# Attention scores on the two row halves of TensorE, a pair's probabilities side by side, and a reordered mixer

## The chip, the cores and the metric

The kernel runs on one core of a Trainium2 chip. The metric is the device time of one execution in microseconds, the median over several runs. One execution was also taken by the hardware profiler; its page, its timeline and its chain of waits are what the prediction reads.

## The reference

The kernel computes two layers of an encoder trunk on 256 tokens of width 1024, all in float32, and a final RMSNorm. Each layer is

```
x += 1/2 SwiGLU_a(RMSNorm(x))
u  = RMSNorm(x) @ W_in          -> q, k, v (512 each), hy (3 * 512)
y_A = neighbourhood attention(q, k, v)      8 heads x 64, bias and mask, softmax
y_B = x0 * long_conv(hv * x1)               512 channels, through a spectrum
x += [RMSNorm(y_A); RMSNorm(y_B)] * g_out @ W_out
x += 1/2 SwiGLU_b(RMSNorm(x))
x += sigmoid(RMSNorm(x) @ W_g) * (p[i] @ W_p)
```

The change lies in the third to fifth line, called the mixer below. For one head of 64 channels the attention computes scores q k^T (256 x 256) times 1/8, adds a bias that is -1e30 outside the neighbourhood, takes a softmax over the keys, and multiplies with v.

## The kernel before

**Products.** Every float32 operand is split into a high part and a rest (`split`, L207: ScalarE rounds, VectorE subtracts), and one product is three matmuls: high by high, high by rest, rest by high. `mm3` (L166 to L170) issues them into one PSUM bank; `Wide.mm` (L187) does the same in the feed-forward parts with one 512-column and one 256-column matmul. Weights stream from HBM: each half piece is loaded, rounded by ScalarE (L281) and its rest taken by VectorE (L283), some six half pieces ahead of their use. Activations lie transposed, channels on partitions and the 256 tokens along the free axis.

**Order of work.** TensorE and ScalarE run in the order in which the program issues instructions; the order on VectorE and GpSimd is a planner's. Side work (normalising, softmax, splitting) stands in generators called fibers. `paced` (L172) counts matmul triples in units of 256 columns; at each third unit `tick` (L150) steps every live fiber once, newest first. `yield` and `rest(n)` in a fiber let it sleep 1 or n ticks. `finish` (L134) ticks until a fiber is done, with no matmul issued in between. So the number of counted units decides between which matmuls a fiber's own TensorE and ScalarE instructions are placed.

**The mixer** (L669). First v for all heads (`vps`, two banks, tokens on partitions). Then the blocks of `ORDER` (L55) one after another. `g`, `q` and `x` are blocks of two products of eight triples each (`columns`, L673), 16 counted units: q and k of a pair of heads, or inputs of the convolution. The others are

- `s` scores of a pair: for each of its two heads two triples (L758). The contraction runs over all 128 partitions; the head's q is padded with zeros in the other head's 64 partitions (`QK`, L718: `qh`, `ql`, zeroed by GpSimd), so the other head's k drops out.
- `t` turn: eight 128 x 128 transposes of the probabilities (L787), one bank per head, then a split per head.
- `p` attend: per head and per half of the keys one triple of 256 columns (L821), four triples into one bank; v is padded with zeros in the other head's columns (`values`, L697).
- `u` turns the convolution's input, `f` is its forward transform with the product in the spectrum (`spectral`, L894), `i` the transform back.

At the end `project` multiplies with W_out in two halves m = 0, 1 of the output channels. A fiber of `Turned` (L952) forms `w` on VectorE (L964, two token halves) and then issues eight transposes on TensorE (L971) into banks, from which VectorE adds to x (L976); `prep` then scales and splits x into the next block's inputs `xg` (L363, L365). The next feed-forward begins at once with `Wide.mm` over its inputs c = 0 to 7, four 512-column matmuls (L188) for each c and, after every second c, eight 256-column ones (L197). c = 0 to 3 come from m = 0, c = 4 to 7 from m = 1; so the eight transposes of m = 1 fall among the first L188 matmuls of that feed-forward.

Of the kernel before, what the change touches and what calls it, by code (L numbers as in the profile page):

```python
# [54 lines left out]
ORDER = "g0 q0 g1 s0 q1 g2 t0 s1 g3 q2 t1 p0 u0 q3 f0 s2 f1 p1 s3 t2 x0 x1 t3 i0 p2 p3 i1 i2 i3"  # L55
MIXER = [(t[0], int(t[1])) for t in ORDER.split()]

# [20 lines left out]
def hybrid_trunk(ctx: ExitStack, tc: tile.TileContext, w, xT, pT, rpb, small, gfin, wf, zT, dft, idft, decay, out):  # L78
# [590 lines left out]
    def mixer(i):  # L669
# [24 lines left out]
        vh = [[t2(F32R, "vh") for _ in range(2)] for _ in range(2)]  # L694
        vl = [[t2(F32R, "vl") for _ in range(2)] for _ in range(2)]

        def values():  # L697
            for tt in range(2):
                for pp in range(2):
                    G.memset(f(vh[tt][pp]), 0.0)  # L700
                    G.memset(f(vl[tt][pp]), 0.0)
            yield from rs.wait()
            for tt in range(2):
                vf = t2()
                V.tensor_scalar(vf, vps[tt], rs.r[:, tt : tt + 1], None, op0=ALU.mult)
                yield
                for pp in range(2):
                    src = vf[:, pp * 256 : (pp + 1) * 256].rearrange("p (a b c) -> p a b c", a=2, b=2)
                    hv, lv = v2(vh[tt][pp]), v2(vl[tt][pp])
                    for par in range(2):  # L710
                        cs = slice(par * 192, par * 192 + 64)
                        S.copy(hv[:, :, cs], src[:, :, par])
                    yield
                    for par in range(2):
                        cs = slice(par * 192, par * 192 + 64)
                        V.tensor_sub(lv[:, :, cs], src[:, :, par], f(hv[:, :, cs]))

        class QK:  # L718


            def __init__(self, b):
                self.kh, self.kl = t1(F32R), t1(F32R)
                self.qh, self.ql = t2(F32R), t2(F32R)
                self.fb = spawn(self.go(b))

            def go(self, b):
                G.memset(f(self.qh), 0.0)
                G.memset(f(self.ql), 0.0)
# [5 lines left out]
                where = [  # L734
                    (slice(64 * par, 64 * par + 64), slice(T * par, T * par + T)) for par in range(2)
                ]
# [619 lines left out]
```

## Time and profile before

| | us |
|---|---|
| median of 3 runs | 1078.4 (1078.39 to 1078.43) |
| the profiled execution | 1078.43, span 1076.7 |
| TensorE (PE) busy | 1057.3 (98%), 6442 matmuls |
| VectorE busy | 876.0 (81%) |
| ScalarE busy | 659.0 (61%) |
| GpSimd busy | 131.1 (12%) |
| mean granted TensorE clock | 0.997 of full speed |

The span is the time between the first and the last instruction of the profile; the execution's own time is 1.7 us longer. The matmuls are pipelined: a row's duration is the time of one from start to end, several are under way at once, and what one costs in a row of them is the distance from one start to the next. The first mixer's blocks run from 211.55 to 297.7 us, the second's from 740.5 to 827.1 us.

### The profile page before, as it was taken

To read this page: it belongs to the slowest core of one execution; us is meant where nothing else is said; L and a number is where in the kernel's file an instruction comes from. 1 tells how busy PE (TensorE), PEld (TensorE's weight loads), DVE (VectorE), ACT (ScalarE), POOL (GpSimd) and SP (SyncE) were. 2 spreads that over 40 slices of the span, in tenths; PEclk is the share of its full clock that TensorE was granted. 3 is DMA by queue.
4 is the path that set the end of the run, shared out by engine and by line. 5 is a ranking of instruction groups with operands and counts; after the bars stand their busy time and mean duration, and the time that the engine had idled before them with its cause. 6 is when DMAs were issued, how large, how long until landed. Compare 5 with 4: busy or idle time off the path is not lost.

```text
span 1076.7 us, 17162 instructions
## 1 busy us (share of the span) xinstructions
PE 1057.3 (98%) x6442; PEld 947.9 (88%) x6442; DVE 876.0 (81%) x1562; ACT 659.0 (61%) x1198; POOL 131.1 (12%) x138
## 2 busy tenths in 40 slices
PE   7999999999999999999999999999999999999996
PEld 6888888899988888888988888889999788888885
DVE  5999878798988877676889888899989887776765
ACT  7566665476766656555667665655767665665553
POOL 3000111511212000010110001223131300000100
PEclk9999999999999999999999999999999999999998
DMA  8666545454345555545465654545523555555541
GB/s 325 212 232 235 197 157 195 176 198 156 118 166 170 187 191 195 196 162 197 152 217 187 234 196 162 191 156 185 198 89 111 177 190 197 182 180 186 173 160 40
DMA packets 33411, 194.54 MB, mean 181 GB/s; under 512 B 3632, under 2 KB 6832, under 8 KB 11312
## 3 DMA queue, kind: packets, MB, share of 16 engines
q1 hardware_dynamic: 33328, 193.44, 51.7%
q8 instruction: 51, 0.84, 0.3%
q14 instruction: 32, 0.26, 0.1%
HBM read 192.38 MB, written 1.05 MB: 180 GB/s over the span
## 4 chain that ended last, share of the span: by engine, by line
PE 94%; DVE 3%; ACT 2%; issue 1%; DMA 0%; SPq 0%; DVEq 0%; ACTq 0%
PE ps L188 44%; PE ps L197 23%; PE ps L167 8%; PE ps L169 8%; PE ps L168 8%; DVE wl L283 1%; DVE xg L365 1%; PE ps L787 1%; ACT wh L281 0%; PE ps L413 0%; DMA raw<-in_w 0%; ACT t L780 0%; DVE x L1076 0%; PE ps L971 0%; DVE s L1075 0%
## 5 line engine op out<-in xcount | busy, mean ns | idle before, releaser
L283 DVE TENSOR_TENSOR wl<-raw,wh 128x1024 fp32r<-128x1024 f32 (+1 forms) x350 | 430.6, 1253 | 105.0 <-PE ps L197 51.5
L281 ACT CAST wh<-raw 128x1024 fp32r<-128x1024 f32 (+1 forms) x350 | 363.4, 1042 | 184.5 <-PE ps L188 90.2
L188 PE MATMUL ps<-xg,wh 128*128 128x512 f32 x1408 | 344.6, 393 | 8.2 <-DVE xg L1195 6.5
L188 PEld LDWEIGHTS ps<-xg,wh 128*128 128x128 f32 x1408 | 258.5, 189 | 58.4 <-DVE xg L1195 6.8
L197 PEld LDWEIGHTS ps<-xg,wl 128*128 128x128 f32 x1408 | 182.4, 192 | 7.7
L197 PE MATMUL ps<-xg,wl 128*128 128x256 f32 x1408 | 184.6, 283 | 0.0
L188 PE MATMUL ps<-act,wh 128*128 128x512 f32 x704 | 173.0, 391 | 0.0
L188 PEld LDWEIGHTS ps<-act,wh 128*128 128x128 f32 x704 | 128.2, 189 | 23.9
L351 POOL TENSOR_TENSOR acc<-acc,q 128x256 f32<-128x256 f32 x56 | 55.9, 999 | 532.1 <-ACT q L348 395.7
L167 PE MATMUL ps<-xg,wh 128*128 128x256 f32 x384 | 109.0, 284 | 0.0
L169 PE MATMUL ps<-xg,wl 128*128 128x256 f32 x384 | 108.7, 283 | 0.0
L168 PE MATMUL ps<-xg,wh 128*128 128x256 f32 x384 | 108.7, 283 | 0.0
L197 PEld LDWEIGHTS ps<-act,wl 128*128 128x128 f32 x704 | 92.9, 191 | 5.1
L197 PE MATMUL ps<-act,wl 128*128 128x256 f32 x704 | 94.4, 282 | 0.0
L202 ACT COPY gu<-ps 128x256 f32<-128x256 f32 x176 | 56.4, 375 | 45.1 <-PE ps L197 45.0
L167 PEld LDWEIGHTS ps<-xg,wh 128*128 128x128 f32 x384 | 73.7, 192 | 0.1
L168 PEld LDWEIGHTS ps<-xg,wh 128*128 128x128 f32 x384 | 73.7, 192 | 0.1
L169 PEld LDWEIGHTS ps<-xg,wl 128*128 128x128 f32 x384 | 73.7, 192 | 0.0
L205 DVE TENSOR_TENSOR gu<-gu,ps 128x256 f32<-128x256 f32 x176 | 66.1, 414 | 0.0
L500 DVE TENSOR_TENSOR act<-s,act 128x256 fp32r<-128x256 f32 x88 | 36.6, 424 | 33.1 <-ACT act L498 32.5
L363 ACT ACTIVATE xg<-x,sm 128x256 fp32r<-128x256 f32 x56 | 27.0, 506 | 35.8 <-DVE x L529 24.3
L365 DVE SCALAR_TENSOR_TENSOR xg<-x,sm,xg 128x256 fp32r<-128x256 f32 x56 | 30.2, 558 | 12.6 <-ACT xg L363 12.4
(209 smaller groups left out, 1236.8 us busy)
## 6 DMA issues: line engine op xcount, KB each, us to landing
raw<-in_w SPq DMA_DIRECT2D x172, 1024.0 KB, 4.9
bias<-in_rpb SPq DMA_DIRECT2D x16, 256.0 KB, 2.7
raw<-in_w SPq DMA_DIRECT2D x4, 256.0 KB, 4.5
x<-in_xT SPq DMA_DIRECT2D x8, 128.0 KB, 4.7
raw<-in_w SPq DMA_DIRECT2D x2, 512.0 KB, 5.7
t<-in_wf SPq DMA_DIRECT2D x4, 256.0 KB, 5.5
dec<-in_decay SPq DMA_DIRECT2D x4, 256.0 KB, 5.5
out<-yo SPq DMA_DIRECT2D x3, 256.0 KB, 2.1
```

Of the source, the lines that this page charges most:

```text
L167: PE.matmul(o, lh, rh, start=start, stop=False)
L168: PE.matmul(o, lh, rl, start=False, stop=False)
L169: PE.matmul(o, ll, rh, start=False, stop=stop)
L188: PE.matmul(b, lh, r, start=start, stop=False)
L197: PE.matmul(o, ll, rh, start=False, stop=stop)
L202: S.copy(dst, b[:, T:])
L205: V.tensor_add(dst, dst, b[:, :T])
L281: S.copy(h[:, a : a + k], src)
L283: V.tensor_sub(l[:, a : a + k], src, f(h[:, a : a + k]))
L351: G.tensor_add(self.ac, self.ac, q)
L365: V.scalar_tensor_tensor(hl[:, T:], x[c], g, f(hl[:, :T]), op0=ALU.mult, op1=ALU.subtract)
L500: V.tensor_sub(hl[:, T:], s, f(hl[:, :T]))
```

## The change

- **Scores.** q and k are no longer padded. A pair's two heads stay in partitions 0 to 63 and 64 to 127, and each matmul contracts over 64 partitions: the two heads' matmuls alternate and write two banks. There are still 12 matmuls of 256 columns for a pair, and the block counts two units instead of four.
- **Turn and attend.** The transposes put the two heads' probabilities side by side, one bank per half of the keys. `attend` multiplies a pair's 128 columns of v with 512 columns of probabilities, six matmuls instead of twelve, and only the two diagonal blocks of the result (64 x 256 each) are copied out by ScalarE before `head_norm`.
- **Values and QK** split 512 columns at once; the zeroing on GpSimd and the small copies go.
- **Spectrum.** One yield less after each pair of multiplications and one less between the GpSimd combination and its split.
- **Order.** The blocks stand in another order, and s0 and s1 now run between the two products of q1 and q2. s2 stands right behind q3, and t2 behind x0.
- **The end.** `rest(1 + m)`: the transposes of m = 1 come one tick later.

```diff
-ORDER = "g0 q0 g1 s0 q1 g2 t0 s1 g3 q2 t1 p0 u0 q3 f0 s2 f1 p1 s3 t2 x0 x1 t3 i0 p2 p3 i1 i2 i3"
+ORDER = "g0 q0 g1 q1+s0 g2 g3 t0 q2+s1 p0 u0 q3 s2 t1 f0 f1 p1 s3 x0 t2 x1 t3 p2 i0 p3 i1 i2 i3"
...
+                S.activation(vh[tt], vps[tt], AF.Copy, scale=r)
+                yield
+                V.scalar_tensor_tensor(vl[tt], vps[tt], r, f(vh[tt]), op0=ALU.mult, op1=ALU.subtract)
...
-                S.copy(self.kh, q[:, T:])
-                for r, c in where:
-                    S.copy(self.qh[r, c], q[r, :T])
-                yield
-                V.tensor_sub(self.kl, q[:, T:], f(self.kh))
-                for r, c in where:
-                    V.tensor_sub(self.ql[r, c], q[r, :T], f(self.qh[r, c]))
+                S.copy(self.h, q)
+                yield
+                V.tensor_sub(self.l, q, f(self.h))
...
-                    mm3(b[:, tt * T : (tt + 1) * T], st.qh[:, qs], st.ql[:, qs], st.kh, st.kl, True, True)
+            banks = [bank(), bank()]
+            for tt in range(2):
+                qs = slice(tt * P, (tt + 1) * P)
+                for n, (a, b) in enumerate(((st.h, st.h), (st.h, st.l), (st.l, st.h))):
+                    for par, o in enumerate(banks):
+                        r = slice(64 * par, 64 * par + 64)
+                        PE.matmul(o[:, tt * T : (tt + 1) * T], a[r, qs], b[r, T:], start=n == 0, stop=n == 2)
+                paced()
...
+            for kt in range(2):
+                b = bank()
+                for h in hs:
+                    h.fb.finish()
+                    for tt in range(2):
+                        o = T * h.par + tt * P
+                        PE.transpose(b[:, o : o + P], h.e[:, tt * T + kt * P : tt * T + (kt + 1) * P], ident)
...
+            for kt, (h, l, fb) in enumerate(ps):
+                fb.finish()
+                vs = slice(128 * pair, 128 * pair + 128)
+                mm3(b, vh[kt][:, vs], vl[kt][:, vs], h, l, kt == 0, kt == 1)
...
+                for par in range(2):
+                    r = slice(64 * par, 64 * par + 64)
+                    S.copy(y[r], b[r, T * par : T * par + T])
...
                 p.append((m, p0, p1))
                 yield
-                yield
...
                 yield
                 yield
-                yield
                 S.copy(yf[m][0], p0)
...
-                yield
+                yield from rest(1 + m)
                 self.banks = [bank(), bank()]
```

## Rows read from the trace of the kernel before

**Rows 1.** The page's first part: engine, busy us, share of the span, instructions.
```profile
PE 1057.3 (98%) x6442; PEld 947.9 (88%) x6442; DVE 876.0 (81%) x1562; ACT 659.0 (61%) x1198; POOL 131.1 (12%) x138
```
**Rows 2.** The page's chain of work that ended last: share of the span by engine.
```profile
PE 94%; DVE 3%; ACT 2%; issue 1%; DMA 0%; SPq 0%; DVEq 0%; ACTq 0%
```
**Rows 3.** Who waited for whom, TensorE alone, the whole span: us in total, times, longest.
```profile
PE ps L188 <- DVE xg L365: 1.8, 2, 1.0
PE ps L971 <- DVE w L964: 1.5, 2, 1.0
```
**Rows 4.** Stretches of 15 us of the first mixer: length, then busy us (instructions) of PE, PEld, DVE, ACT, POOL, then the granted TensorE clock, the DMA share and GB/s.
```profile
220.00:235.00 15.00, 15.00 (x127) 15.00 (x127) 14.91 (x28) 10.67 (x21) 1.21 (x2) 1.00 0.59 216
...
265.00:280.00 15.00, 14.86 (x101) 13.35 (x100) 14.14 (x27) 9.72 (x28) 5.83 (x5) 1.00 0.42 141
```
**Rows 5.** Timeline of TensorE, the scores of the first pair: the first of its 12 matmuls, and the first matmul behind them. Columns: start us, us, engine, line, operation, out<-in, weights, moving operand, count.
```profile
229.06 0.28 PE L167 MATMUL ps<-s,t 128*128 128x256 f32 x1
...
230.50 0.28 PE L167 MATMUL ps<-xg,wh 128*128 128x256 f32 x1
```
**Rows 6.** Timeline of TensorE, the transposes of the first pair (eight, merged into a row) and the two matmuls behind them.
```profile
242.02 1.04 PE L787 MATMUL ps<-ident,t 128*128 128x128 f32 x8
242.81 0.36 PE L167 MATMUL ps<-s,t 128*128 128x256 f32 x1
243.02 0.28 PE L168 MATMUL ps<-s,t 128*128 128x256 f32 x1
```
**Rows 7.** Timeline of TensorE: two 512-column matmuls three apart, then the first of the second pair's 12 matmuls with v and the first matmul behind them.
```profile
266.24 0.39 PE L167 MATMUL ps<-t,dft_h 128*128 128x512 f32 x1
...
266.92 0.39 PE L167 MATMUL ps<-t,dft_h 128*128 128x512 f32 x1
...
271.78 0.28 PE L167 MATMUL ps<-t,vh 128*128 128x256 f32 x1
...
273.22 0.28 PE L167 MATMUL ps<-s,t 128*128 128x256 f32 x1
```
**Rows 8.** Timeline of TensorE around the transposes of the third pair, in the first and in the second layer.
```profile
274.67 1.74 PE L787 MATMUL ps<-ident,t 128*128 128x128 f32 x8
276.17 0.36 PE L167 MATMUL ps<-xg,wh 128*128 128x256 f32 x1
...
803.54 0.28 PE L169 MATMUL ps<-s,t 128*128 128x256 f32 x1
803.94 1.92 PE L787 MATMUL ps<-ident,t 128*128 128x128 f32 x8
805.61 0.36 PE L167 MATMUL ps<-xg,wh 128*128 128x256 f32 x1
```
**Rows 9.** Timeline of ScalarE just there, second layer: the four scalings of the third pair's probabilities.
```profile
803.38 1.87 ACT L780 ACTIVATE t<-t,ri 128x256 f32<-128x256 f32 x4
```
**Rows 10.** Timeline of TensorE at the end of the first mixer: the transposes of m = 1 among the first L188 matmuls (in brackets idle us and what ended it); the row at 328.60 begins with c = 4.
```profile
320.90 1.07 PE L188 MATMUL ps<-xg,wh 128*128 128x512 f32 x4
321.81 0.27 PE L971 MATMUL ps<-ident,w 128*128 128x128 f32 x1
323.11 0.98 PE L971 MATMUL ps<-ident,w 128*128 128x128 f32 x7 [1.03 <-DVE w L964]
323.85 1.17 PE L188 MATMUL ps<-xg,wh 128*128 128x512 f32 x4
...
328.60 2.00 PE L188 MATMUL ps<-xg,wh 128*128 128x512 f32 x8
```
**Rows 11.** The same at the end of the second mixer; the row at 858.40 begins with c = 4.
```profile
850.33 1.53 PE L188 MATMUL ps<-xg,wh 128*128 128x512 f32 x6
851.70 0.27 PE L971 MATMUL ps<-ident,w 128*128 128x128 f32 x1
852.45 0.98 PE L971 MATMUL ps<-ident,w 128*128 128x128 f32 x7 [0.48 <-DVE w L964]
853.19 0.71 PE L188 MATMUL ps<-xg,wh 128*128 128x512 f32 x2
...
858.40 2.11 PE L188 MATMUL ps<-xg,wh 128*128 128x512 f32 x8 [0.76 <-DVE xg L365]
```
**Rows 12.** Timeline of VectorE at the end of the first mixer.
```profile
322.31 0.74 DVE L964 SCALAR_TENSOR_TENSOR w<-ps,rt,w 128x512 f32<-128x512 f32 x1
...
326.12 1.66 DVE L365 SCALAR_TENSOR_TENSOR xg<-x,sm,xg 128x256 fp32r<-128x256 f32 x4
```
**Rows 13.** Timeline of VectorE at the end of the second mixer.
```profile
851.65 0.74 DVE L964 SCALAR_TENSOR_TENSOR w<-ps,rt,w 128x512 f32<-128x512 f32 x1
...
856.21 2.14 DVE L365 SCALAR_TENSOR_TENSOR xg<-x,sm,xg 128x256 fp32r<-128x256 f32 x4
```
**Rows 14.** Groups of instructions by line from 205 to 310 us, that is the first mixer: line, engine, operation, shapes, count, then busy us, mean ns of one, then idle us before them.
```profile
L168 PE MATMUL ps<-s,t 128*128 128x256 f32 x16 | 4.5, 282 | 0.0
...
L743 DVE TENSOR_TENSOR t<-t,t 64x256 fp32r<-64x256 f32 x8 | 3.3, 417 | 0.1
...
L168 PEld LDWEIGHTS ps<-s,t 128*128 128x128 f32 x16 | 3.1, 191 | 0.0
...
L732 DVE TENSOR_TENSOR t<-ps,rb 128x512 f32<-128x512 f32 x4 | 2.7, 680 | 0.0
...
L716 DVE TENSOR_TENSOR vl<-t,vh 128x128 fp32r<-128x128 f32 x8 | 2.1, 288 | 0.0
```

More of the change, by code (lines that the diff above doesn't have):

```diff
@@ L751, in __init__, with scored @@
                 nc.sync.dma_start(self.bias, rpb[i, 2 * pair + par])
-            def scores(self, st):
-                st.fb.finish()
-                b = bank()
-                for tt in range(2):
-                    qs = slice(T * self.par + tt * P, T * self.par + (tt + 1) * P)
-                    mm3(b[:, tt * T : (tt + 1) * T], st.qh[:, qs], st.ql[:, qs], st.kh, st.kl, True, True)
+            def scored(self, b):
                 self.e = t2()
@@ L997, in mixer, with emit @@
         vfb = spawn(values())
-        qs, hs = {}, {}
-        for kind, j in MIXER:
+        qs, hs, ps, stats = {}, {}, {}, {}
+        def emit(kind, j, between=None):
             if kind == "g":
-                gated(j, columns())
+                gated(j, columns(between))
             elif kind == "q":
-                qs[j] = QK(columns())
+                qs[j] = QK(columns(between))
             elif kind == "x":
-                outer(2 * j, columns())
+                outer(2 * j, columns(between))
             elif kind == "s":
@@ L1008, in mixer @@
             elif kind == "t":
-                turn(hs[j])
+                ps[j] = turn(hs.pop(j))
             elif kind == "p":
-                attend(j, hs.pop(j))
+                attend(j, ps.pop(j))
                 if len(yna) == 4:
-                    na = Rstd(None, nsq.parts, HY, [fb for _, fb in yna], STAT_NA)
+                    stats["na"] = Rstd(None, nsq.parts, HY, [fb for _, fb in yna], STAT_NA)
             elif kind == "u":
@@ L1020, in mixer @@
                 if len(yhy) == 4:
-                    hy = Rstd(None, hsq.parts, HY, [fb for _, fb in yhy], STAT_HY)
-        behind = [spawn(first(m, project(m, yna), na)) for m in range(2)]
+                    stats["hy"] = Rstd(None, hsq.parts, HY, [fb for _, fb in yhy], STAT_HY)
+        for block, *inner in MIXER:
+            emit(*block, (lambda: emit(*inner[0])) if inner else None)
+        behind = [spawn(first(m, project(m, yna), stats["na"])) for m in range(2)]
         new_norm()
         for m in range(2):
-            turned = Turned(m, project(m, yhy), hy, behind[m])
+            turned = Turned(m, project(m, yhy), stats["hy"], behind[m])
             for c in range(4 * m, 4 * m + 4):
@@ L1277, in _weights @@
         put(win[8:12].transpose(1, 0, 2, 3))
[L1278 removed]
+        for (kind, j), *_ in MIXER:
             if kind in "gqx":
```

79 lines of the change are left out of this document (21 added, 58 removed).

## The prediction, made before the changed kernel ran

> **What bounds the kernel now.** I read the page's engine shares first: TensorE is busy for 98% of the span, VectorE for 81%, ScalarE for 61% [rows 1]. The chain of waits says the same: 94% of it is TensorE's own instructions [rows 2]. The stretches of the mixer show how dense that is: TensorE is busy for 15.00 of 15 us with the granted clock at 1.00, while VectorE reaches 14.91 in one stretch [rows 4]. So the time is nearly the sum of TensorE's steps from start to start, plus a few waits. The list of waits names two places in the part that the change touches, both at the end of a mixer: 1.5 us for `w` and up to 1.8 us for `xg` [rows 3]. A third place hides in the durations of merged rows (below). VectorE is close behind, so each edit is also asked for what it adds there.
>
> **Scores.** A pair's 12 matmuls of 256 columns take 230.50 - 229.06 = 1.44 us, 0.12 each [rows 5]. After the change there are 12 again, each on 64 of the 128 rows, alternating between the halves. The trace holds no matmul of 64 rows. From below: both halves run side by side, six steps of 0.12, 0.72 us. From above, for matmuls that stay hidden behind one another: no overlap at all, 1.44. To this comes a change of the array's shape ahead of and behind each block. The nearest row to that is the step from transposes to matmuls: the first matmul behind them takes 243.02 - 242.81 = 0.21 us instead of 0.12, 0.09 more [rows 6]; two per pair make 0.18. I take side by side with both switches, 0.90 us, because the two heads share neither rows nor a bank: 0.54 us less per pair, 8 pairs in the two layers, **-4.3 us**. Without switches it would be -5.8; one after the other with them, +1.4.
>
> The Trainium skill, page TensorEngine Tiling (Array Packing), section Key Properties, says that changing the tiling mode drains TensorE, and names no price. No run here shows it. By that rule the dearer switch would be a whole lone matmul's tail, 0.28 - 0.12 = 0.16 us, and the scores would save 0.40 instead of 0.54 per pair, 1.1 us less in all.
>
> **Attend.** 12 matmuls of 256 columns take 273.22 - 271.78 = 1.44 us; three steps of 512 columns take 266.92 - 266.24 = 0.68, 0.227 each [rows 7]. Six of them make 1.36: 0.08 less, 8 times, **-0.6 us**. The cross blocks that nobody reads cost no more than the zeros did. The two copies that ScalarE adds per pair (some 0.4 us each, by the 64 x 256 subtraction's 417 ns on VectorE [rows 14]) lie behind TensorE's next block: the result is wanted only by `project`, at least three `i` blocks later.
>
> **Turn.** Eight transposes before, eight after, 0.79 us with the step behind them [rows 6]: nothing. But the third pair's do not take 0.79. In the first layer they hold TensorE for 276.17 - 274.67 = 1.50 us; in the second from 803.66 (0.12 behind the start at 803.54) to 805.61, 1.95 us [rows 8]. They wait for the softmax: ScalarE's four scalings start only at 803.38 and last 1.87 us [rows 9]. In the old order t2 comes 16 units behind s2 (f1, p1, s3), 5 ticks, and the softmax fiber needs 7, so `finish` ticks on with no matmul between. In the new order s2 and t2 lie t1, f0, f1, p1, s3 and x0 apart: 8 + 8 + 4 + 2 + 16 = 38 units, 12 ticks. The other pairs have 13 (t0), 10 (t1) and 10 (t3). Both waits go: 0.71 + 1.16 = **-1.9 us**. Next latest is u0: g3's fiber needs 7 ticks and has 22 units, against 20 before, where nothing waited. p3 stays 8 units behind t3.
>
> **The extra rest.** First layer: from the first transpose of m = 1 to the next L188 row are 323.85 - 321.81 = 2.04 us, 1.25 over the 0.79 [rows 10, 6], because the second `w` ends at 322.31 + 0.74 = 323.05 [rows 12]. Counting the ticks: these transposes came behind the 4th L188 matmul, so ticks fell at 1, 4, 7. Each pair's scores now count two units less, eight in a layer, which moves ticks by 8 - 6 = 2 positions, to 3, 6, 9; with the extra rest it is the 9th, behind the first eight L197 matmuls too: 320.90 + 9 x 0.227 + 8 x 0.12 = 323.9. `w` is there, the wait is gone. Late next is c = 4: newest fibers step first, so its `xg` is the last of four and ends at 326.12 + 1.66 = 327.78 [rows 12]. TensorE would want it at 328.60 - 1.25 = 327.35 and waits 0.43: **-0.8 us** remain. Second layer: the transposes move from the 6th to the 7th L188 matmul (sixteen units less, one position). They lose 853.19 - 851.70 - 0.79 = 0.70 us now [rows 11], but behind them TensorE already waits for the same `xg`, which ends at 856.21 + 2.14 = 858.35 [rows 13]. The chain through `w` (851.65 + 0.74) is not shorter, so what is saved at the first wait is waited at the second: 0. Bounds: both layers' waits go altogether, -0.43 and -0.70 - 0.76 more, -2.7; or VectorE's planner puts a 1.65 us L283 ahead of the sums, +1.
>
> **Values, QK, spectrum.** None of it is on TensorE. VectorE loses two subtractions of 0.417 us per pair and eight of 0.288 per layer, and keeps one of 512 columns for each, some 0.68 by the nearest 512-column row [rows 14]; so it gets no busier, and the zeroing leaves GpSimd, which is busy 12% [rows 1]. They hide behind TensorE's blocks; were that cover gone, the whole is below 3 us a layer. The spectrum's fewer yields bring a result that is wanted 42 units later (p1, s3, x0, x1, p2 between f1 and i0); ScalarE may stand behind GpSimd for some tenths, behind six half pieces of weights in stock. 0, at most +-0.5.
>
> **Sum.** -4.3 - 0.6 - 1.9 - 0.8 = -7.6 us against the profiled execution's 1078.43 (span 1076.7 and 1.7 around it), which is the median too: 1070.8.
>
> **The rivals.**
> 1. *The halves run one after the other.* Each 64-row matmul has its own weight load, and a load of 128 columns may not overlap the other half's. The transposes show such a bound: with 128 columns they step at 0.79 / 8 = 0.099 us, not at half of 0.12 [rows 6]. Then 12 x 0.099 + 0.18 = 1.37 or 12 x 0.12 + 0.18 = 1.62 us per pair, -0.6 or +1.4 in all; with the other -3.3 it is 1074.5 to 1076.5, middle 1075.5. For it: the loads are as many as before, 88% of the span [rows 1]. Against it: they overlap matmuls everywhere now. The Trainium skill, page TensorE: Matmul & The Clock Gate, section LDWEIGHTS, says that a load's time goes by the columns and not by the rows, which would leave a half's load as long as a whole one; it bears on this rival alone, and no row here shows a half's load.
> 2. *Slower: loads on the halves are not hidden at all.* If a half's next load starts only when its matmul has ended, a step is 0.19 + 0.28 = 0.47 us [rows 14], and even with two halves at once a pair takes 6 x 0.47 = 2.82 us, +1.38, 8 times +11.0: with -3.3, 1086.1. It decides from a mean step of (1.44 + 3.3 / 8) / 12 = 0.154 us on. Against it: now every load runs ahead of its matmul.
> 3. *The waits only move.* The new order puts a wait of t2's size, 0.71 and 1.16 us, somewhere else (u0, p3, or a bank that VectorE frees late, at 14.1 to 14.9 of 15 us busy [rows 4]): the -1.9 goes, 1072.7. It lies in the likeliest one's range.
>
> **How the numbers follow.** Side by side, with or without new small waits: 0.62, at 1070.8, from 1068.5 (no switches, -5.8, and part of the end's bound) to 1073. One after the other: 0.27. Loads exposed: 0.06. Other losses that I do not see (a worse chain at the end, a wait in each block): 0.05. The range 1068.5 to 1076.5 takes in the first two. This kernel's runs can tell 0.2%, 2.2 us, from no change. Faster by more than that is all of the first and 0.6 of the second: 0.78. Within it are the rest of the second and a little of the others, 0.13; slower 0.09.
>
> **What would show it.** Between the first and the last start of a pair's score matmuls some 0.7 us instead of 1.32, with the two halves starting close together; if the starts are 0.10 to 0.12 apart, rival 1 holds; at 0.15 or more, rival 2. Attend rows 0.227 apart. The transposes of t2 back at 0.79 us in both layers. At the end no wait for `w` in the first layer, and a wait for `xg` at c = 4 in both. Wrong I would be if other waits for ScalarE or VectorE appear between 210 and 300 us, or if the mixer's blocks do not shorten from 86.2 and 86.6 us to some 83.0 (scores -2.2, attend -0.3, t2 -0.7 and -1.2).

## The result: 3.5 us slower, and the profile after

The changed kernel takes 1081.87 us (median of 5 runs, 1081.81 to 1083.53) against 1078.41 for the kernel before: a ratio of 1.0038, 95% interval 1.0027 to 1.0049. The forecast was 1070.8, with a range up to 1076.5. The profiled execution took 1081.84, its span is 1080.0.

The page of the changed kernel: engine, busy us, share of the span, instructions; then the chain of waits that ended last, by engine.

```profile
PE 1054.7 (98%) x6394; PEld 940.5 (87%) x6394; DVE 868.2 (80%) x1530; ACT 659.4 (61%) x1186; POOL 120.2 (11%) x106
...
PE 63%; DVE 5%; ACT 1%; issue 1%; DVEq 0%; ACTq 0%
```

TensorE is busy 2.6 us less than in [rows 1], VectorE 7.8 us less, GpSimd 10.9 us less, and the span is 3.4 us longer (1080.04 against 1076.65). The work did shrink; what grew is time in which TensorE waits, or runs at a lower clock. The list of waits names the places (TensorE's waits: us in total, times, longest):

```profile
PE ps L189 <- DVE xg L366: 4.3, 3, 2.3
PE ps L169 <- DVE t L210: 3.0, 2, 2.0
PE ps L168 <- ACT t L209: 0.6, 1, 0.6
PE ps L954 <- DVE w L947: 0.3, 1, 0.3
```

L189 waiting for `xg` was 1.8 us in [rows 3] and is 4.3; the wait for `w` was 1.5 and is 0.3. The second and third row are new: L168 and L169 are the matmuls of `mm3`, L209 and L210 are `split`, and it is the attend block p3 that asks for t3's probabilities.

**Where the 3.4 us come from.** Cut at fixed instructions of TensorE's timeline, the span divides like this. A mixer runs from its first `xg` matmul to the first L189 behind `project`; its end runs from there to the fourth group of L198 (inputs c = 6 and 7); the tail runs from the last matmul's start to the end of the span.

| us | before | after | difference |
|---|---|---|---|
| first mixer | 109.35 | 108.31 | -1.04 |
| end of the first mixer | 12.33 | 12.57 | +0.24 |
| second mixer | 109.79 | 110.16 | +0.37 |
| end of the second mixer | 12.81 | 15.78 | +2.97 |
| tail | 9.41 | 10.56 | +1.15 |
| all else | 822.96 | 822.66 | -0.30 |

The gain is in the mixers, and part of it is eaten there. Start with what went well. Timeline of TensorE, changed kernel: the scores of the first pair, with the matmuls ahead and behind.

```profile
231.72 0.28 PE L170 MATMUL ps<-xg,wl 128*128 128x256 f32 x1
231.93 0.39 PE L855 MATMUL ps<-t 64*128 64x256 f32 x2
232.15 0.40 PE L855 MATMUL ps<-t,t 64*128 64x256 f32 x4
232.39 0.28 PE L855 MATMUL ps<-t 64*128 64x256 f32 x2
232.51 0.40 PE L855 MATMUL ps<-t,t 64*128 64x256 f32 x4
232.84 0.39 PE L168 MATMUL ps<-xg,wh 128*128 128x256 f32 x1
233.06 0.28 PE L169 MATMUL ps<-xg,wh 128*128 128x256 f32 x1
```

The two halves run side by side: their matmuls start in pairs (rows of x2 and x4). Without the block the next matmul would have started at 231.72 + 0.12 = 231.84; it starts at 232.84, and its own step is 0.22 instead of 0.12. So a pair takes 1.00 + 0.10 = 1.10 us: 0.72 for six steps of 0.12 and 0.38 for the two changes of shape, half of it on each side: 0.09 ahead of the block and 0.10 on its own first step (232.15 - 231.93 = 0.22), and as much behind it. Before it took 1.44 [rows 5].

The transposes of the third pair are back at the 0.79 us of [rows 6] in both layers, where they held TensorE for 1.50 and 1.95 us [rows 8]; the second layer's, with the first matmul behind them:

```profile
806.79 1.03 PE L836 MATMUL ps<-ident,t 128*128 128x128 f32 x8
807.58 0.36 PE L168 MATMUL ps<-xg,wh 128*128 128x256 f32 x1
```

**First loss: p3.** The same timeline a little later, first and second layer (idle us and what ended it in brackets):

```profile
289.08 0.39 PE L168 MATMUL ps<-t,vh 128*128 128x512 f32 x1
290.52 0.50 PE L169 MATMUL ps<-t,vh 128*128 128x512 f32 x1 [1.04 <-DVE t L210]
...
291.78 0.28 PE L168 MATMUL ps<-idft_h,t 128*128 128x256 f32 x1
...
817.00 0.28 PE L170 MATMUL ps<-idft_h,t 128*128 128x256 f32 x1
817.88 0.50 PE L168 MATMUL ps<-t,vh 128*128 128x512 f32 x1 [0.60 <-ACT t L209]
820.38 0.50 PE L169 MATMUL ps<-t,vh 128*128 128x512 f32 x1 [2.00 <-DVE t L210]
...
821.66 0.28 PE L168 MATMUL ps<-idft_h,t 128*128 128x256 f32 x1
```

The block should take six steps of 0.227, 1.36 us. It takes 291.78 - 289.08 = 2.70 and, from 817.00 + 0.12, where it could have started, 821.66 - 817.12 = 4.54: 1.34 and 3.18 us lost. The idle times in brackets are smaller: they count from the modelled end of a matmul, not from where the next could have started, and the matmul behind a pause has a longer step as well (0.33 us from 290.52 on). VectorE in the second layer shows what it did meanwhile:

```profile
813.39 1.29 DVE L210 TENSOR_TENSOR t<-ps,t 128x512 fp32r<-128x512 f32 x2 [1.44 <-ACT t L209]
...
818.12 1.21 DVE L284 TENSOR_TENSOR wl<-raw,wh 128x1024 fp32r<-128x1024 f32 x1
819.25 0.47 DVE L802 SCALAR_TENSOR_TENSOR x<-t,sm,x 128x255 f32<-128x255 f32 x1
819.65 1.28 DVE L210 TENSOR_TENSOR t<-ps,t 128x512 fp32r<-128x512 f32 x2
```

A weight subtraction (L284) and a step of the convolution stand ahead of t3's rest. The row at 813.39 is t2's rest; VectorE had been idle for 1.44 us before it, for ScalarE's cast, and from there on it has no idle time until t3's rest is done.

**Second loss: the end of the second mixer.** Timeline of TensorE, to be held against [rows 11]; then the granted clock there (columns as in [rows 4]):

```profile
859.12 3.03 PE L189 MATMUL ps<-xg,wh 128*128 128x512 f32 x8 [2.32 <-DVE xg L366]
861.95 1.79 PE L198 MATMUL ps<-xg,wl 128*128 128x256 f32 x8
```

```profile
860.00:862.00 2.00, 2.00 (x7) 1.51 (x6) 1.35 (x2) 0.00 (x0) 0.00 (x0) 0.51 0.27 45
862.00:864.00 2.00, 2.00 (x11) 1.95 (x10) 0.17 (x1) 1.04 (x1) 0.00 (x0) 0.64 0.83 299
```

The wait at c = 4 grew from 0.76 to 2.32 us. Behind it the clock is granted at 0.51 and 0.64, about its lower level of 1.2 GHz instead of 2.4: eight L189 take 861.95 - 859.12 = 2.83 us; at the full clock they take 1.84 (below, c = 4 scaled first). VectorE at the same place:

```profile
851.96 1.65 DVE L284 TENSOR_TENSOR wl<-raw,wh 128x1024 fp32r<-128x1024 f32 x1 [0.17 <-ACT wh L282]
853.53 1.40 DVE L959 TENSOR_TENSOR x<-x,ps 128x256 f32<-128x256 f32 x4
854.85 1.21 DVE L284 TENSOR_TENSOR wl<-raw,wh 128x1024 fp32r<-128x1024 f32 x1
855.99 3.08 DVE L366 SCALAR_TENSOR_TENSOR xg<-x,sm,xg 128x256 fp32r<-128x256 f32 x4
```

Two weight subtractions stand around the sums L959, and c = 4's `xg`, the last of four, comes at 859.07. Those four took 2.14 us before [rows 13] and 1.66 in the first mixer [rows 12]; here they take 3.08. The first takes 0.47 us and the other three 0.94 or 0.95, each beside a sum of squares on GpSimd (L352, 0.8 us each).

**Third loss: the tail.** ScalarE behind the last matmul, first in the kernel before (last start at 1067.24), then in the changed one (last start at 1069.47). The sigmoid of the last part is L1127 in the former and L1114 in the latter; the square for the final norm is L1135 and L1122.

```profile
1067.97 0.46 ACT L1127 ACTIVATE t<-ps,rt 128x256 f32<-128x256 f32 x1
1068.33 0.40 ACT L1135 ACTIVATE t<-t 128x256 f32<-128x256 f32 x1
```

```profile
1071.00 0.40 ACT L1122 ACTIVATE t<-t 128x256 f32<-128x256 f32 x1
...
1071.40 0.45 ACT L1114 ACTIVATE t<-ps,rt 128x256 f32<-128x256 f32 x1
```

Before, the sigmoid came first and began 0.73 us behind the last matmul's start; now the square of the part before it comes first, and the sigmoid begins 1.93 us behind. The ticks fall between other matmuls than before, 220 us behind the end of the second mixer.

### The profile page after: what moved, and what is told of

It reads as the page before. It is cut to its first block, busy times and chain, and to the rows that moved or that the text cites. A ratio compares the mean times of both kernels' runs of the same rounds, so it can differ in the third digit from the quotient of the medians.

```text
span 1080.0 us, 16967 instructions
## 1 busy us (share of the span) xinstructions
PE 1054.7 (98%) x6394; PEld 940.5 (87%) x6394; DVE 868.2 (80%) x1530; ACT 659.4 (61%) x1186; POOL 120.2 (11%) x106
## 3 DMA queue, kind: packets, MB, share of 16 engines
HBM read 192.38 MB, written 1.05 MB: 179 GB/s over the span
## 4 chain that ended last, share of the span: by engine, by line
PE 63%; DVE 5%; ACT 1%; issue 1%; DVEq 0%; ACTq 0%
PE ps L189 33%; PE ps L198 17%; PE ps L168 4%; PE ps L169 4%; PE ps L170 4%; DVE wl L284 1%; DVE xg L366 1%; ACT t L754 0%; DVE t L210 0%; DVE s L1062 0%; DVE x L1063 0%; PE ps L855 0%; PE ps L414 0%; DVE t L740 0%; DVE x L959 0%
## 5 line engine op out<-in xcount | busy, mean ns | idle before, releaser
L284 DVE TENSOR_TENSOR wl<-raw,wh 128x1024 fp32r<-128x1024 f32 (+1 forms) x350 | 429.4, 1250 | 115.9 <-ACT wh L282 57.0
L189 PE MATMUL ps<-xg,wh 128*128 128x512 f32 x1408 | 345.5, 394 | 10.9 <-DVE xg L1182 6.6
L189 PEld LDWEIGHTS ps<-xg,wh 128*128 128x128 f32 x1408 | 258.7, 189 | 61.9 <-DVE xg L1182 7.5
L198 PEld LDWEIGHTS ps<-xg,wl 128*128 128x128 f32 x1408 | 182.5, 192 | 7.7
L198 PE MATMUL ps<-xg,wl 128*128 128x256 f32 x1408 | 184.5, 283 | 0.0
L189 PE MATMUL ps<-act,wh 128*128 128x512 f32 x704 | 173.2, 391 | 0.0
L189 PEld LDWEIGHTS ps<-act,wh 128*128 128x128 f32 x704 | 128.2, 189 | 23.8
L352 POOL TENSOR_TENSOR acc<-acc,q 128x256 f32<-128x256 f32 x56 | 57.9, 1034 | 527.8 <-ACT q L349 374.6
L168 PE MATMUL ps<-xg,wh 128*128 128x256 f32 x384 | 109.8, 286 | 0.0
L169 PE MATMUL ps<-xg,wh 128*128 128x256 f32 x384 | 108.6, 283 | 0.0
L198 PEld LDWEIGHTS ps<-act,wl 128*128 128x128 f32 x704 | 92.9, 191 | 5.1
L198 PE MATMUL ps<-act,wl 128*128 128x256 f32 x704 | 94.4, 282 | 0.0
L168 PEld LDWEIGHTS ps<-xg,wh 128*128 128x128 f32 x384 | 73.7, 192 | 0.9
L169 PEld LDWEIGHTS ps<-xg,wh 128*128 128x128 f32 x384 | 73.7, 192 | 0.1
```

The costliest lines, as they stand in the source:

```text
L168: PE.matmul(o, lh, rh, start=start, stop=False)
L169: PE.matmul(o, lh, rl, start=False, stop=False)
L189: PE.matmul(b, lh, r, start=start, stop=False)
L198: PE.matmul(o, ll, rh, start=False, stop=stop)
L284: V.tensor_sub(l[:, a : a + k], src, f(h[:, a : a + k]))
L352: G.tensor_add(self.ac, self.ac, q)
```

## The experiments

All times are medians beside runs of the kernel before on the same chip (1078.3 to 1078.5), with the ratio to it and its interval. A kernel named without a base is the changed one with the edit shown.

**One rest again.** Does the extra rest cost?

```diff
-                yield from rest(1 + m)
+                yield from rest(1)
```

> One edit on the changed kernel (1081.9 us): the extra rest is taken back, rest(1) for both halves. Theory A (c = 4 waits for xg at the end of VectorE's chain, so the place of the transposes decides nothing): the wait for w grows, the wait for xg shrinks by as much, time within 0.5 us of 1081.9. Rival B (the extra rest itself pushes the chain back by a tick, which makes the longer wait and then the slower clock in the second layer): the transposes come some 0.7 to 1.6 us earlier, the clock stays at 1.00 there, and the time falls by 1.5 to 3 us, to 1079 to 1080.4.

1079.84 us, 1.0013 (1.0004 to 1.0022): 2.0 us less than the changed kernel. The waits for `w` are back (0.48 and 1.02 us), the wait at c = 4 is 0.77 us in the first layer and none in the second, and the clock behind the second mixer is 1.00. So the rest moved a wait from `w` to c = 4 and made it longer. On VectorE the 1.65 us weight subtraction stands ahead of the sums of the second layer here too, but none stands between the sums and `xg`, and each of the four `xg` takes 0.47 us. Behind p3 in the second layer this execution has a stretch at half clock, which the changed kernel has not.

**p3 one block later.** Is the distance between t3 and p3 the cause?

```diff
-ORDER = "... t3 p2 i0 p3 i1 i2 i3"
+ORDER = "... t3 p2 i0 i1 p3 i2 i3"
```

> One edit on the changed kernel (1081.9 us): p3 moves behind i1 (t3 p2 i0 i1 p3 i2 i3), 1.4 us more between the last turn and the matmuls that want its split. Theory A (p3 stands too close behind t3, now that ScalarE and VectorE run late there): of the 1.3 us (first layer) and 3.2 us (second layer) that p3's block takes too long, about 1.3 and 1.4 go, so -2.7 us at the ffn's first matmul, 1079.2 +- 1 at the end. Rival B (VectorE is the bound of this stretch): the wait turns up at the next place that needs VectorE, and the time stays within 0.7 us of 1081.9.

1082.4 us, 1.0038 (1.0023 to 1.0053): no gain. In the first layer p3 no longer waits, but 1.46 us of waiting for GpSimd's sum of squares come instead, at 299.38, with a low clock behind; in the second layer p3 still waits 1.43 us. Distance helps p3, and the next late thing takes its place.

**Scores counted as four units.** The arithmetic stays; the ticks behind each mixer fall where they fell before.

```diff
-                paced()
+                paced(2)
```

> One edit on the changed kernel (1081.9 us): a pair's scores count four units again instead of two, so that all ticks behind a mixer fall where they fell before the change. Theory A (the phase of the ticks costs the end of the second mixer and the tail behind the last matmul): the tail is back at the length of before (-1.1 us behind the last matmul, -0.6 ahead of it) and the ends of the mixers change, 1079.5 +- 1. Rival B (the phase is of no account): same time within 0.5 us, with the waits where they are.

1079.02 us, 1.0009 (0.9999 to 1.0018). The tail is 9.44 us again, as before the change (9.41). Timeline of ScalarE, last matmul starting at 1069.67: the sigmoid is ahead of the square again and begins 0.73 us behind it.

```profile
1070.40 0.45 ACT L1114 ACTIVATE t<-ps,rt 128x256 f32<-128x256 f32 x1
1070.76 0.40 ACT L1122 ACTIVATE t<-t 128x256 f32<-128x256 f32 x1
```

p3 waits 1.90 us in the first layer and not at all in the second, whose mixer takes 107.35 us; c = 4 waits 2.34 and 1.25 us.

**The new arithmetic in the old order.**

```diff
-ORDER = "g0 q0 g1 q1+s0 g2 g3 t0 q2+s1 p0 u0 q3 s2 t1 f0 f1 p1 s3 x0 t2 x1 t3 p2 i0 p3 i1 i2 i3"
+ORDER = "g0 q0 g1 s0 q1 g2 t0 s1 g3 q2 t1 p0 u0 q3 f0 s2 f1 p1 s3 t2 x0 x1 t3 i0 p2 p3 i1 i2 i3"
```

> The changed kernel with the order of blocks of before: scores on row halves, side by side probabilities and shorter spectrum stay. Theory A (the new order makes p3's wait): p3's wait goes (-4.5 us), the third pair's wait at its transposes comes back (+1.9), 1079 +- 1, and less if the end does not suffer. Rival B (the new split and the copies of attend make it): p3 still waits, 1082 or more.

1087.48 us, 1.0087 (1.0072 to 1.0102), the worst of all. p3 doesn't wait; the transposes of t2 wait for the softmax, 2.73 and 2.47 us, longer than in the kernel before. Behind the first of these waits the clock is granted at 0.73 and 0.50. TensorE now reaches t2 sooner, and s3 counts two units less between s2 and t2; the run doesn't part the two. The new order is needed with the new arithmetic.

**The new order alone**, on the kernel before (its padded scores and twelve-matmul attend).

```diff
-ORDER = "g0 q0 g1 s0 q1 g2 t0 s1 g3 q2 t1 p0 u0 q3 f0 s2 f1 p1 s3 t2 x0 x1 t3 i0 p2 p3 i1 i2 i3"
+ORDER = "g0 q0 g1 q1+s0 g2 g3 t0 q2+s1 p0 u0 q3 s2 t1 f0 f1 p1 s3 x0 t2 x1 t3 p2 i0 p3 i1 i2 i3"
```

> The kernel before (1078.4 us) with the new order of the blocks alone: s0 and s1 between the products of q1 and q2, and so on; scores padded over 128 rows, one bank per head, the old spectrum, one rest. Theory A (the order makes p3's wait, the faster scores only sharpen it): the third pair's waits go (-1.9 us), p3 waits in at least one layer, 1077 to 1079.5. Rival B (the wait needs the new arithmetic, which gives the other engines less time): no wait at p3, 1076.5 or less.

1077.81 us, 0.9994 (0.9985 to 1.0003). t2's waits are gone, p3 waits 0.79 us in the first layer only, the end of the mixers is as in [rows 10, 11]. So the order takes away 1.9 us and gives back 0.8 even without the new arithmetic; the rest of p3's loss comes only with the rest of the change. Which part of that brings it, this run does not show.

**The halves issued one after the other**, three matmuls of one and then three of the other.

```diff
-                for n, (a, b) in enumerate(((st.h, st.h), (st.h, st.l), (st.l, st.h))):
-                    for par, o in enumerate(banks):
+                for par, o in enumerate(banks):
+                    for n, (a, b) in enumerate(((st.h, st.h), (st.h, st.l), (st.l, st.h))):
```

> One edit on the changed kernel: the three matmuls of one half are issued in a row and then the three of the other, instead of alternating. Theory A (only neighbouring matmuls on different halves run side by side): a pair's scores take 12 x 0.12 us and the two switches, 1.6 to 1.75 us instead of 1.00, and the whole is some 3 to 6 us slower unless waits take it up. Rival B (the order inside a block is of no account, TensorE looks further ahead): 1.0 to 1.2 us per pair.

One run: 1082.1 us, span 1080.3. Timeline of TensorE, to be held against the same block of the changed kernel above:

```profile
232.23 0.39 PE L855 MATMUL ps<-t 64*128 64x256 f32 x2
232.45 0.40 PE L855 MATMUL ps<-t,t 64*128 64x256 f32 x4
232.69 0.29 PE L855 MATMUL ps<-t 64*128 64x256 f32 x2
232.81 0.41 PE L855 MATMUL ps<-t,t 64*128 64x256 f32 x4
233.14 0.39 PE L168 MATMUL ps<-xg,wh 128*128 128x256 f32 x1
```

The row of two at 232.23 holds the first matmul of each half (high by high, one operand name), though the second of them is issued as the fourth. The two start 10 ns apart here and 3 ns in the changed kernel, so the order of issue did change. The block takes the same 1.00 us. The halves proceed independently; the order of issue between them doesn't matter here.

**c = 4 scaled first** at the end of each mixer, instead of last: the four fibers that scale a half's inputs are started in reverse.

```diff
-            for c in range(4 * m, 4 * m + 4):
+            for c in reversed(range(4 * m, 4 * m + 4)):
                 onward(i, C_FFB, c, turned.add(c))
+            scaled[-4:] = scaled[:-5:-1]
```

> One edit on the changed kernel (1081.9 us): of the four inputs that each half of the last projection yields, the one that TensorE wants first (c = 0, c = 4) is scaled and split first instead of last; nothing else moves. Theory A (the wait at c = 4 is the place of c = 4 in VectorE's queue, last of four, each some 0.55 us): c = 4 comes 1.2 to 1.7 us earlier, the waits at c = 4 shrink from 1.24 and 2.32 us to 0 to 0.8 in both layers, the granted clock stays at 1.00 behind the second mixer (1 to 1.6 us more), sum -2.5 to -4 us: 1078 to 1079.4. Rival B (the whole of VectorE is late there): the wait goes to c = 5 or 6, and the time stays within 0.7 us of 1081.9.

1077.5 us, 0.9989 (0.9979 to 0.9998): 4.4 us less than the changed kernel. Timeline and clock at the end of the second mixer:

```profile
857.75 2.00 PE L189 MATMUL ps<-xg,wh 128*128 128x512 f32 x8
859.59 1.12 PE L198 MATMUL ps<-xg,wl 128*128 128x256 f32 x8
```

```profile
860.00:862.00 2.00, 2.00 (x13) 1.74 (x13) 1.43 (x2) 1.99 (x5) 0.00 (x0) 1.00 0.84 356
```

No wait at c = 4, no lower clock: the ends take 11.21 and 11.53 us (after: 12.57 and 15.78). p3 still waits (1.02; 0.59 and 2.00). The ten executions spread from 1075.97 to 1078.22, and the profiled one, 1075.99, is among the shortest; what lengthens the others is not shown.

**The same on the kernel before**, to see how much of it belongs to the change.

> The kernel before, with c = 4 scaled first at the end of each mixer and nothing else. Theory A: the wait for c = 4's input belongs to the order in which the four inputs are scaled, and not to the change; the kernel before loses only 0.76 us to it, in the second layer, and its waits for w (1.03 and 0.48 us) lie ahead of it and stay: 1077.4 to 1078.0, so the gain of 4.4 us in the changed kernel is what the extra rest had put there. Rival B: scaling c = 4 first also frees VectorE for w or keeps the clock up, and gives the kernel before as much as the changed one: 1075 or less.

1077.19 us, 0.9990 (0.9980 to 0.9999): 1.1 us less. The 0.76 at c = 4 is gone, and the waits for `w` are 0.36 + 0.33 and 0.26 instead of 1.03 and 0.48. Theory A wanted 1077.4 to 1078.0 and unchanged waits for `w`: these shrank too, and the time is 0.2 below its range, but far from rival B's 1075. So about 1.1 of the 4.4 us had been there before the change; 3.3 were added by it.

**t3's split stepped first** among the fibers, ahead of the convolution and the weights.

```diff
-                made.append((h, l, spawn(go(), True)))
+                made.append((h, l, spawn(go())))
```

> One edit on the changed kernel (1081.9 us): the fiber that splits the turned probabilities is stepped first in its tick instead of last, so ScalarE rounds them ahead of the weight casts and of the convolution of that tick. Theory A (p3 waits because ScalarE does other work of the same tick first): p3's waits (1.3 us in the first layer, 3.2 in the second) fall by 1 us or more each, 1079 +- 1. Rival B (VectorE's queue is late by itself, whatever ScalarE does): ScalarE's rounding comes earlier, VectorE's subtraction does not, and p3 waits as long: within 0.7 us of 1081.9.

1083.82 us, 1.0053 (1.0038 to 1.0068). p3's waits are 0.98 and 0.26 + 1.79 us, nearly as they were: ScalarE's cast comes sooner in the second layer (0.26 instead of 0.60), VectorE's rest doesn't. So far rival B holds, but the time is 1.9 us above the changed kernel, outside both theories. The transposes of t3 now wait for the softmax in both layers: from the first of them to the next matmul it takes 1.72 and 1.71 us instead of 0.80 and 0.79, of which the list of waits shows 0.2. Behind p3 in the second layer the clock is granted at 0.83, 0.50 and 0.82, which the changed kernel has not. Making the cast earlier is not the cure.

**Work taken off VectorE.** On the kernel with c = 4 first, the spectrum's split subtraction goes to GpSimd.

```diff
-                V.tensor_sub(yf[m][1], p0, f(yf[m][0]))
+                G.tensor_sub(yf[m][1], p0, f(yf[m][0]))
```

> The changed kernel with c = 4 scaled first, and with the spectrum's split subtraction on GpSimd instead of VectorE (four 512-column instructions of some 0.68 us per mixer leave VectorE's queue). Theory A: p3's wait (1.3 us in the first mixer, 3.2 us in the second) comes from VectorE being late with its queue around 270 to 290 us; with 2.7 us off that queue per mixer, the rest of t3's split is there earlier, the wait goes in the first mixer and falls to 1 us or less in the second, and the time is some 3 us below that of the kernel with c = 4 first alone: 1074 to 1075. Rival B: the order is at fault (p3 stands 8 units behind t3, and ScalarE's cast alone comes too late, or GpSimd is slower and i0 then waits for the spectrum): p3's two waits stay at 1.0 and 2.0 us or a new one appears, and the time stays at 1077 to 1079.

1076.17 us, 0.9979 (0.9969 to 0.9988). p3's waits are 0.59 and 0.68 + 1.40 us: shorter by 0.43 and 0.51, where theory A wanted the first gone and the second at 1 or less. The time lies between the two theories. So VectorE's load matters, but 2.7 us of it taken away bought half a us at p3 in each layer. A likely reason, not tested alone, lies in VectorE's timeline around 280 us:

```profile
278.68 4.14 DVE L284 TENSOR_TENSOR wl<-raw,wh 128x1024 fp32r<-128x1024 f32 x2
...
282.88 1.26 DVE L210 TENSOR_TENSOR t<-ps,t 128x512 fp32r<-128x512 f32 x2
...
284.67 1.95 DVE L284 TENSOR_TENSOR wl<-raw,wh 128x1024 fp32r<-128x1024 f32 x1
```

and in GpSimd's:

```profile
279.45 4.54 POOL L896 TENSOR_TENSOR t<-t,t 128x512 fp32r<-128x512 f32 x2
284.24 1.30 POOL L896 TENSOR_TENSOR t<-t,t 128x512 fp32r<-128x512 f32 x1 [0.26 <-ACT t L894]
```

The two L284 at 278.68 take 4.14 us together and the one at 284.67 takes 1.95, where two in a row take 2.34 in the changed kernel (at 279.69) and one takes 1.21; the pair that reads a PSUM bank (L210) keeps its time. The Trainium skill, page GPSIMD Engine Reference, section Specifications, says that GpSimd's way to SBUF is shared with VectorE, and contended when VectorE's instruction has two SBUF inputs. L284 has two, L210 has one, and this stretch agrees. It does not happen each time: of the 36 weight subtractions of this execution that lie for more than half of their time beside an instruction of GpSimd, 23 keep 1.21 to 1.27 us, and no run shows what decides. Behind the wait in the second layer the clock is granted at 0.50, which lengthens this execution's mixer by a us.

**The weight subtraction behind t3's rest.** The direct test: on the kernel with c = 4 first, a weight piece's subtraction is held back by up to three ticks between x1 and p3.

```diff
                 S.copy(h[:, a : a + k], src)
                 yield
+                for _ in range(3):
+                    if Stream.late:
+                        yield
                 V.tensor_sub(l[:, a : a + k], src, f(h[:, a : a + k]))
...
+            Stream.late = block in (('x', 1), ('t', 3), ('p', 2), ('i', 0), ('p', 3))
```

> The changed kernel with c = 4 scaled first, and the weights' subtraction held back by up to three ticks between x1 and p3. On TensorE and ScalarE every instruction keeps its place; on VectorE one 1.2 us weight subtraction, which in the second layer stood right ahead of t3's rest, comes behind it; in the first layer the order stays. Theory A (VectorE's queue order): the second layer's wait for the rest falls from 2.00 us by the subtraction's step of 1.14 us to some 0.9, the 0.59 ahead of it (ScalarE's cast) stays, and the first layer's 1.02 stays; the time falls by about 1 us, from 1077.5 to 1076.5. Rival B (the rest is late for another reason: the cast, the banks, or VectorE waiting for ScalarE): the second layer's wait stays at 1.8 us or more.

1075.38 us, 0.9971 (0.9960 to 0.9982). Second layer, VectorE and then TensorE:

```profile
817.58 1.28 DVE L210 TENSOR_TENSOR t<-ps,t 128x512 fp32r<-128x512 f32 x2
...
819.38 1.47 DVE L288 TENSOR_TENSOR wl<-raw,wh 128x1024 fp32r<-128x1024 f32 x1
```

```profile
816.95 0.50 PE L168 MATMUL ps<-t,vh 128*128 128x512 f32 x1 [0.60 <-ACT t L209]
818.33 0.50 PE L169 MATMUL ps<-t,vh 128*128 128x512 f32 x1 [0.87 <-DVE t L210]
```

The weight subtraction (L288 here) is behind the rest, and the wait fell from 2.00 to 0.87 us, by the 1.13 that the subtraction occupied. The first layer, whose order on VectorE stayed, still waits 1.05. The second mixer takes 109.01 us instead of 110.14. That is theory A, to the hundredth at the wait; the median fell by 2.1 us, more than it accounts for. The shortest executions of the two kernels differ by 1.2 us (1075.97 and 1074.80), which it does account for; the profiled spans differ by 0.5 us, with a start that is 0.6 later here.

**c = 4 first, and scores counted as four.**

> The changed kernel with c = 4 scaled first, and with a pair's scores counted as four units again, as before the change, so that every later block of the kernel meets the ticks at the old places. Theory A: two independent mends, so their gains add up: c = 4's waits (1.2 and 2.3 us and the half clock behind the second) are gone, the end of the kernel is 1.1 us shorter (10.55 to 9.4 us behind the last matmul), and p3's waits in the two mixers together stay at about 3 us: 1075 to 1076. Rival B: the tick places decide p3's wait by chance as much as anything, and the waits in the mixers grow by what the end gives back: 1077 to 1079.

1074.73 us, 0.9964 (0.9950 to 0.9978). The two gains add up; the tail is 9.4 us. p3 waits 1.90 us in the first layer only.

**All three:** c = 4 first, GpSimd for the spectrum's split, scores counted as four.

> The changed kernel with all three: c = 4 scaled first, the spectrum's split subtraction on GpSimd, and a pair's scores counted as four units. Theory A: the forecast of 1070.8 lacked only the waits that the change put on new places (p3, c = 4, the end behind the last matmul); with all three away the time comes to 1071 to 1074. Rival B: VectorE's queue is late as a whole in the mixers, and any wait that is taken away comes back at the next block: 1076 to 1078.

1071.93 us, 0.9943 (0.9928 to 0.9957). The mixers take 107.87 and 107.01 us; what is left is 0.58 us at p3 in the first layer.

**The same, with the rests last in attend:** both halves' high parts first, then the two matmuls on the probabilities' rests.

```diff
-                mm3(b, vh[kt][:, vs], vl[kt][:, vs], h, l, kt == 0, kt == 1)
+                PE.matmul(b, vh[kt][:, vs], h, start=kt == 0, stop=False)
+                PE.matmul(b, vl[kt][:, vs], h, start=False, stop=False)
+                paced(2)
+            for kt, (h, l, fb) in enumerate(ps):
+                PE.matmul(b, vh[kt][:, 128 * pair : 128 * pair + 128], l, start=False, stop=kt == 1)
```

> The changed kernel with c = 4 scaled first, the spectrum's split on GpSimd, the scores counted as four units, and attend's six matmuls ordered so that the two on the probabilities' rests come last. Theory A (p3's wait is for the rest alone, and the order within the block does not matter otherwise): the rest is wanted 0.68 us later, so the 0.58 us in the first layer goes or is below 0.2, the second layer stays without a wait, and the time is 1071 to 1073, the forecast's 1070.8 missed only by the dearer switch of the scores. Rival B (the block that waits is one of many that VectorE is late for): the wait comes back at i1 or at the next block, and the time is 1072.5 or more.

1071.51 us (1071.27 to 1071.70), 0.9935 (0.9922 to 0.9947): the best, 6.9 us below the kernel before and 10.4 below the changed one. TensorE's waits from the list, which now has none at p3 (the row of `xg` lies between 500 and 600 us, outside the mixers and their ends, and was there before):

```profile
PE ps L189 <- DVE xg L366: 1.0, 1, 1.0
PE ps L958 <- DVE w L951: 0.2, 1, 0.2
```

The chain of waits is TensorE's own work again, for 93% (63% in the changed kernel, 94% in [rows 2]).

## Why the prediction was wrong

| term, us | predicted | in the changed kernel |
|---|---|---|
| scores | -4.3 | -2.7 (8 x (1.44 - 1.10)) |
| attend | -0.6 | about -0.2 |
| t2's waits | -1.9 | -1.9 |
| p3's new wait | 0 | +4.5 (1.34 + 3.18) |
| extra rest and the ends | -0.8 | +3.2 (0.24 + 2.97) |
| tail | not considered | +1.15 |

The right column sums to +4.1 against a span that grew by 3.4; the 0.3 of "all else" and some tenths in the mixers are not placed one by one.

**Scores: the mechanism right, the switches mis-sized.** Side by side it is, in 0.72 us. Two switches were put at 0.09 each, after the step from transposes to matmuls [rows 6]. They measure 0.19 each, 0.38 together: the longer first step that this row shows (0.10 here) and, ahead of it, a gap of 0.09, which the row does not have and the sum lacked. The Trainium skill, page TensorEngine Tiling (Array Packing), section Key Properties, says that changing the tiling mode drains TensorE; the prediction's sum by that rule allowed 0.32 for both, and the trace stands nearer to that than to the 0.18 that was taken. Rivals 1 and 2 fell: the matmuls start two at a time, pairs 0.12 apart, and the loads of both halves (0.18 us each) are hidden.

**Attend: small either way.** Start to start, the four blocks of the second layer take 5.82 us before and 5.71 with all waits gone (the kernel with all three edits), so 0.03 per pair were saved instead of 0.08.

**t2: right**, both waits, to the hundredth. The new order does what was read from the tick counts.

**The step that failed first: "p3 stays 8 units behind t3", "Next latest is u0", and the cover for VectorE's work.** The 8 units are right, and u0 does not wait. But units count TensorE's work, and p3 does not wait for ticks: it waits for VectorE's queue, in which the planner puts a 1.2 us weight subtraction ahead of t3's rest. The prediction noted that VectorE gets no busier and took that for safety. The load was indeed no higher: from 803 to 818 us VectorE is busy for 12.10 of 15 us, against 14.59 before. And in the kernel with all three edits it is busy for 14.80 in the same stretch, and p3 does not wait there. What counts is the order in the queue over the last few us. The runs: moving only that subtraction took 1.13 of the 2.00 us; the new order alone, on the old arithmetic, loses 0.8 us there; the new arithmetic in the old order loses it at t2. The other waits of p3 (0.60 for ScalarE's cast, the 0.87 that is left, 1.04 in the first layer) are read from the timelines and not taken away one by one. That TensorE reaches p3 sooner by what it saved is an argument and not shown: with the scores counted as four units the same arithmetic has no wait in the second layer. The prediction's own sign of being wrong, other waits for ScalarE or VectorE in the mixer, is what came. Rival 3 had the mechanism and two of its places, p3 and VectorE, with a price of at most the 1.9 us that it was to take back. The price had no such bound.

**The extra rest: the chain was followed only through `w`.** In the first layer `w`'s wait went, as predicted, behind the first eight L198, and c = 4 came next, but with 1.24 us instead of 0.43: the sums, which the later transposes feed, start 0.90 us later than before, counted from the first L189 (L188 before), and `xg` with them; the prediction had left `xg` where it was. In the second layer the saving was called 0 because `xg` would end at the same time. Counted from the first L189 it ends 1.42 us later (859.07 - 849.63 against 858.35 - 850.33). A part is the 1.65 us weight subtraction ahead of the sums, which start 0.76 us later: the bound of +1 us named in the prediction and not taken. The other part had no term at all: three of the four `xg` take twice their time beside GpSimd, where one did before, 0.94 us more. With one rest the subtraction ahead of the sums is there as well, and c = 4 does not wait; so by the two timelines what the extra rest costs here is the subtraction between the sums and `xg`, and the meeting with GpSimd. The wait of 2.32 us was then followed by the lower clock, which the prediction never considered. With one rest again the kernel is 2.0 us faster, with c = 4 scaled first 4.4 us.

**The tail was left out.** The prediction counted ticks up to the end of the mixers. The count carries on to the end of the kernel, and there it swapped a sigmoid and a square on ScalarE: +1.15 us, undone by counting the scores as four units again.

What the forecast called the likeliest sum was within reach of the arithmetic: with c = 4 first, GpSimd for one subtraction, the old tick count and the rests last, the kernel takes 1071.5 against the 1070.8 that was forecast. But that is another kernel, and about 1.1 us of its gain (c = 4 on the kernel before) have nothing to do with the change.

Still open: why p3 waits in the one layer or the other as the count of ticks changes (with the scores counted as four units the second layer has no wait and the first a longer one), why a pause is sometimes followed by the lower clock and sometimes not, and when VectorE and GpSimd slow each other down.

## What to carry to other kernels

When the engine that bounds the time gets faster and a second engine is 80% busy or more beside it, ask of every handover not only how far it lies behind in the first engine's work, but what stands ahead of it in the second one's queue: each such place can cost a whole instruction of that queue, 1.1 us here, and a mean load that does not grow is no cover. An edit that takes counted steps out of a schedule moves every later decision that is made by the count; look at the tail and at the far end too, or keep the count as it was while the arithmetic changes. A rest that is added to take away one wait should be followed to the last consumer, since the next wait can be longer and bring the clock down.

## What the runs showed of the hardware

- Two 64-row halves of TensorE run independently: both begin together even when three matmuls of one half are issued first, and twelve matmuls of 256 columns take six steps. Going in and out of that shape cost 0.38 us per block, 0.19 on each side.
- Behind a pause of 2.32 us the granted clock was 0.51 and then 0.64, over 4 us. Behind the pauses of 0.60 and 2.00 us at p3 in the same execution it stayed at 1.00; in the kernel with one rest, behind the same 0.60 and 2.00 us, it was 0.83, 0.50 and 0.81; with the spectrum's split on GpSimd, behind 0.68 and 1.40 us, it was 0.75, 0.50 and 0.89 (means of 2 us each). A wait's price is therefore not its own length alone, and the same wait does not always bring it.
- A VectorE instruction with two SBUF inputs can take far longer beside GpSimd's: a weight subtraction 1.95 us instead of 1.21, an `xg` 0.94 instead of 0.47. The split's subtractions, which have a PSUM input, kept their step of 0.6 us. Most weight subtractions beside GpSimd kept their time too.
